# Pairing 64-deep TensorE products in the two halves of the array's rows, in an encoder layer

## The chip, the core and the metric

The kernel runs on one core of one Trainium2 chip: TensorE (PE) for products and transposes, VectorE (DVE), ScalarE (ACT) and GpSimd (POOL) for everything elementwise, SyncE (SP) for issuing most DMAs. Each engine works through its own list of instructions in order and waits on semaphores for the others. The metric is the device time of one execution in microseconds (us); less is better.

## What is computed

One layer: a token mixer made of sparse attention (8 heads, keys chosen by an "indexer") and differential attention (4 heads), then attention into 256 memory tokens, then a mixture of 64 experts. 512 tokens, width 1024, float32. The parts that the change touches:

```python
# indexer: 8 heads of depth 64, one key per token, one weight per query and head
rel    = relu(einsum('bqhd,bsd->bqhs', qib, k_idx) * IDX_DIM ** -0.5)
iscore = einsum('bqh,bqhs->bqs', wib, rel)
_, sel = top_k(iscore, topk)                       # 128 keys for each query
q_lat  = einsum('bqhd,hcd->bqhc', qb, w_uk)        # depth 64, latent of 128
# differential attention: two softmax maps of depth 64 for each of 4 heads
s1 = einsum('bqhd,bshd->bhqs', q1b, k1) * scale + bias
s2 = einsum('bqhd,bshd->bhqs', q2b, k2) * scale + bias
attn = softmax(s1) - lam * softmax(s2)
# mixture of experts: sums start at zero, each expert's rows are added
acc = zeros((n + 1, d)); acc = acc.at[rows].add(yb)
```

## The kernel before

**Products.** For accuracy every float32 operand is split into a high and a low part (`split`: ACT casts the high part, DVE or POOL subtracts to get the low one). A product is then three matmuls into one PSUM bank (`mm3`, L100 to L103): high by high (L101), high by low (L102), low by high (L103).

**Stages.** In order of time: normalisation of the input and its transposes (to about 30 us); 22 projections by 128 columns of `w_in` (thread `dense`, tile `whl` for the split weights) with the indexer's keys and head weights first (`index_keys`), then the four indexer queries `qi0` to `qi3`, the latent, and queries, keys and values of the four differential heads; beside them `index_scores`, `select` (16 rounds of MAX and MATCH_REPLACE on DVE for each of three blocks of queries) and `head_scores`; 16 projections of the memory tokens (`memh`, `meml`) as work between; the sparse attention (`latent_up`, `sparse_scores`, `sparse_out`); output projection, memory attention, routing; from about 600 us the experts, whose weights stream from HBM, three loads of 1024 KB for each of the 64; at the end the sums and a last normalisation.

**Depth 64.** The array has 128 rows and these products need 64. The indexer and the latent fill the other 64 with zeros: `kz` holds the keys once in rows 0 to 63 and once in rows 64 to 127, zeros elsewhere, and `ukz` likewise (both with `fill0`, memsets on DVE); a matmul then uses all rows. `head_scores` gives each of the two maps (`v`) of a head its own half of the rows, without zeros, three matmuls of one half, then, in another step, three of the other.

**Head weights.** The 8 columns of head weights have a projection of their own after that of the keys (tile `ww`, L330, 24 matmuls of 384 columns), then a scale on ACT (`wit`, L331) and three transposes (L335), ahead of the projection of `qi0`.

**Order.** `schedule` (L117) runs the threads as generators. Each step yields two numbers, TensorE time and a delay until the thread's next step may come; the planner keeps a clock from them and calls the first thread that is due. So the program's order comes from these planned numbers; the chip then runs each engine's list in that order, and the tile library adds the waits. A raw weight chunk is loaded two items ahead by SP into one of three buffers and split one item ahead into one of two; eight PSUM banks and six work buffers (`wk`) turn over.

**Zeros.** `clear_sums` stores zeros into the sums in HBM, 12 stores of 256 KB from `zrow`, issued by POOL in one step once the latent's keys (`ckt`) are there. The first scatter into the sums comes after 620 us.

## Time and profile before

| | |
|---|---|
| time, median of 3 runs | 1300.02 us (1300.02, 1294.96, 1300.17) |
| the profiled execution | 1294.74 us, of it 1292.9 us span |
| busy in the span | PE 89%, DVE 58%, ACT 44%, POOL 35% |
| chain that ended last, by engine | PE 33%, DMA 15%, DVE 7% |
| HBM | read 290 MB, written 38 MB |

The span runs from the first to the last instruction; 1.8 us lie around it. "Busy" of PE counts a matmul from its start to a modelled end, and matmuls overlap, so what a matmul costs in a row of them is read from start to start, not from its length. The share of busy time is a mean over stages with different limits: it is read by stretches. The chain that ended last is followed back from the last instruction; it names what each step waited for.

### The profile page before, as it was taken

The numbers are of one execution on the slowest core, as the hardware profiler recorded it, in microseconds if no ns is written. First come the engines' busy times: TensorE is split into PE (matmuls) and PEld (weight loads), VectorE is DVE, ScalarE is ACT, GpSimd is POOL, SyncE is SP. The second block draws the span as 40 slices with busy tenths as digits, with TensorE's granted clock in tenths as the row PEclk, the third lists the DMA queues.
The fourth block names the chain that finished last, engine by engine and source line by source line (L and its number), as shares of the span: only waits on it lengthen the run. The fifth ranks groups of instructions, "written<-read, shape, count | busy, mean of one in ns | idle before, by whom it ended". The sixth has DMA issues, their size and how long they took to land.

```text
span 1292.9 us, 20999 instructions
## 1 busy us (share of the span) xinstructions
PE 1154.6 (89%) x7768; PEld 911.3 (70%) x7768; DVE 752.4 (58%) x1607; ACT 562.6 (44%) x1006; POOL 451.4 (35%) x346
## 2 busy tenths in 40 slices
PE   2999999999899799988999999999999988798870
PEld 2887778898789799877877777777777544454330
DVE  7267995556773747697776767676575311211115
ACT  3234546654554353443555555556464112312122
POOL 4353344552225343363322222222223222222223
PEclk9998999999989899999999999999999988899895
DMA  7352132554416235787999999999999999999985
GB/s 226 81 180 66 49 98 78 143 183 139 144 50 212 61 123 194 252 317 255 312 305 332 345 350 353 348 353 365 363 365 357 348 371 366 358 364 370 374 278 199
DMA packets 138183, 324.09 MB, mean 251 GB/s; under 512 B 13520, under 2 KB 96464, under 8 KB 113248
## 3 DMA queue, kind: packets, MB, share of 16 engines
q1 hardware_dynamic: 120560, 277.93, 59.1%
q0 software_dynamic: 14432, 44.12, 14.1%
q8 instruction: 62, 1.02, 0.3%
q10 hardware_dynamic: 3088, 0.69, 0.2%
q14 instruction: 41, 0.34, 0.1%
HBM read 290.19 MB, written 37.81 MB: 254 GB/s over the span
## 4 chain that ended last, share of the span: by engine, by line
PE 33%; DMA 15%; DVE 7%; issue 3%; ACT 2%; POOL 1%; SPq 0%; DVEq 0%; ACTq 0%; POOLq 0%
PE ps L1360 9%; DMA wraw<-in_e_w_up_dram 6%; PE ps L101 5%; PE ps L102 5%; PE ps L103 5%; DMA wraw<-in_e_w_gate_dram 4%; PE ps L1313 4%; DVE whl L1277 3%; DMA wd<-in_e_w_down_dram 3%; PE ps L1285 2%; PE ps L1324 2%; DMA acc<-y,sidx 1%; PE ps L1226 1%; DVE h2p L202 1%; ACT whl L1276 1%
## 5 line engine op out<-in xcount | busy, mean ns | idle before, releaser
L95 POOL TENSOR_TENSOR whl<-wraw,whl 128x1024 fp32r<-128x1024 f32 x81 | 196.1, 2421 | 265.4 <-ACT whl L94 230.9
L1277 DVE TENSOR_TENSOR whl<-wraw,whl 128x1024 fp32r<-128x1024 f32 x152 | 182.8, 1229 | 65.2 <-ACT whl L1276 64.7
L101 PE MATMUL ps<-whl,xt 128*96 128x256 f32 (+4 forms) x640 | 183.9, 287 | 3.9 <-ACT whl L1276 3.9
L1252 POOL DMA_INDIRECT xg<-rows,sidx x66 | 80.6, 1222 | 297.9 <-PE ps L1301 135.2
L102 PE MATMUL ps<-whl,xt 128*96 128x256 f32 (+4 forms) x640 | 179.2, 280 | 0.6 <-DVE whl L1277 0.6
L103 PE MATMUL ps<-whl,xt 128*96 128x256 f32 (+4 forms) x640 | 179.2, 280 | 0.0
L1276 ACT CAST whl<-wraw 128x1024 fp32r<-128x1024 f32 x152 | 152.4, 1055 | 11.6 <-DMA wraw<-in_e_w_gate_dram 11.3
L1366 POOL DMA_INDIRECT acc<-y,sidx x66 | 97.4, 1476 | 168.2 <-ACT y L1361 113.6
L1360 PE MATMUL ps<-wd,ht 128*96 128x512 f32 (+4 forms) x320 | 145.8, 598 | 2.8 <-DVE ht L1348 1.9
L1313 PE MATMUL ps<-wraw,xn 128*64 128x256 f32 (+1 forms) x832 | 117.1, 404 | 24.4 <-DMA wraw<-in_e_w_up_dram 8.8
L1332 ACT ACTIVATE sg<-ps 64x256 f32<-64x256 f32 (+6 forms) x66 | 25.0, 379 | 242.4 <-PE ps L1313 127.2
L94 ACT CAST whl<-wraw 128x1024 fp32r<-128x1024 f32 x91 | 95.4, 1049 | 56.2 <-PE ps L103 40.5
L101 PEld LDWEIGHTS ps<-whl,xt 128*96 128x96 f32 (+4 forms) x640 | 104.3, 163 | 4.6 <-ACT whl L1276 4.1
L102 PEld LDWEIGHTS ps<-whl,xt 128*96 128x96 f32 (+4 forms) x640 | 104.4, 163 | 1.0 <-DVE whl L1277 0.7
L103 PEld LDWEIGHTS ps<-whl,xt 128*96 128x96 f32 (+4 forms) x640 | 104.2, 163 | 0.3
L1313 PEld LDWEIGHTS ps<-wraw,xn 128*64 128x64 f32 (+1 forms) x832 | 61.2, 139 | 61.1 <-DMA wraw<-in_e_w_up_dram 12.4
L1360 PEld LDWEIGHTS ps<-wd,ht 128*96 128x96 f32 (+4 forms) x320 | 49.3, 163 | 69.9 <-issue 64.6
L1348 DVE COPY ht<-ps 128x128 f32<-128x128 f32 (+6 forms) x66 | 21.4, 324 | 94.2 <-PE ps L1346 94.1
L1361 ACT COPY y<-ps 96x512 f32<-96x512 f32 (+4 forms) x80 | 46.6, 583 | 67.7 <-PE ps L1360 67.5
L1337 DVE SCALAR_TENSOR_TENSOR hm<-ps,og,sg 64x256 f32<-64x256 f32 (+4 forms) x54 | 36.8, 682 | 60.4 <-ACT sg L1332 47.9
L101 PE MATMUL ps<-xTh,whl 128*128 128x512 f32 (+1 forms) x168 | 66.6, 396 | 0.0
L102 PE MATMUL ps<-xTl,whl 128*128 128x512 f32 (+1 forms) x168 | 64.8, 386 | 0.0
(420 smaller groups left out, 2780.4 us busy)
## 6 DMA issues: line engine op xcount, KB each, us to landing
wraw<-in_e_w_gate_dram SPq DMA_DIRECT2D x64, 1024.0 KB, 23.3
wraw<-in_e_w_up_dram SPq DMA_DIRECT2D x64, 1024.0 KB, 24.2
wd<-in_e_w_down_dram SPq DMA_DIRECT2D x64, 1024.0 KB, 23.2
wraw<-in_w_in_dram SPq DMA_DIRECT2D x21, 512.0 KB, 3.8
wraw<-in_m_wkv_dram SPq DMA_DIRECT2D x16, 512.0 KB, 4.3
wraw<-in_m_wq_dram SPq DMA_DIRECT2D x16, 512.0 KB, 4.0
wraw<-in_m_wo_dram SPq DMA_DIRECT2D x16, 512.0 KB, 4.0
wraw<-in_w_o_dram SPq DMA_DIRECT2D x12, 512.0 KB, 3.5
```

Source lines behind the costliest of these rows:

```text
L94: nc.scalar.copy(hi, src)
L95: eng.tensor_sub(lo, src, hi.bitcast(F32))
L101: nc.tensor.matmul(ps, lhsT=a, rhs=b, start=start, stop=False)
L102: nc.tensor.matmul(ps, lhsT=a, rhs=bl, start=False, stop=False)
L103: nc.tensor.matmul(ps, lhsT=al, rhs=b, start=False, stop=stop)
L1252: nc.gpsimd.indirect_dma_start(out=xg[0:n, :], out_offset=None, in_=rows, in_offset=bass.IndirectOffsetOnAxis(ap=gi[0:n, :], axis=0), boun ...
L1276: nc.scalar.copy(hi[v], w[i][v])
L1277: lo_eng.tensor_sub(lo[v], w[i][v], hi[v].bitcast(F32))
L1313: nc.tensor.matmul(ps[HALF * i:HALF * i + n, 0:256], lhsT=xt[:, k, 0:n], rhs=w[i][:, k, :], start=k == 0, stop=k == KD - 1)
L1360: nc.tensor.matmul(ps[0:n, :], lhsT=ht[:, j, 0:n], rhs=wd[:, j, cs], start=j == 0, stop=j == 1)
L1361: nc.scalar.copy(y[0:n, cs], ps[0:n, :])
L1366: nc.gpsimd.indirect_dma_start(out=accs[(NB - m) % 2], out_offset=bass.IndirectOffsetOnAxis(ap=si[0:n, :], axis=0), in_=y[0:n, :], in_offs ...
```

## The change

1. A new helper `mm3_halves` takes two products, one for each half of the rows, and issues their six matmuls in turn: half 0, half 1, half 0, ... into two banks. `index_scores` (two heads at a time), `head_scores` (both maps of a head) and `latent_up` (two heads) use it.
2. The indexer's keys are kept once in rows 0 to 63 (`kd`) and copied to rows 64 to 127 by a DMA on POOL's queue; `uk` holds two heads in the two halves. The zeros of `kz` and `ukz` go, and half of their splits' instructions.
3. The keys' projection has 72 columns: 64 of keys and the 8 head weights. The separate projection of head weights goes. `index_split` splits two halves of 4 x 72 columns, with the low parts on DVE.
4. The zeros are stored by SP's queue, one store a step, with a planned delay of 1.5 us between them.
5. The planned numbers of these threads change with the steps, and with them the order of everything up to the memory attention.

```diff
+    def mm3_halves(pss, ops):
+
+        for i, j in ((0, 2), (0, 3), (1, 2)):
+            for ps, op in zip(pss, ops):
+                nc.tensor.matmul(ps, lhsT=op[i], rhs=op[j], start=i + j == 2, stop=i == 1)
+
+    HALVES = (slice(0, 64), slice(64, 128))
...
     def index_split(raw):
...
-        for j in range(2):
-            js = slice(j * 64, (j + 1) * 64)
-            split(hl[:, 0, :, js], hl[:, 1, :, js], raw[:, :, 0:64], lo_eng=nc.vector if j else nc.gpsimd)
-        ww = wk([P, 2, KD, 8], F32R, name="ww")
-        split(ww[:, 0], ww[:, 1], raw[:, :, 64:72])
+        for k in (slice(0, 4), slice(4, 8)):
+            split(hl[:, 0, k, 0:72], hl[:, 1, k, 0:72], raw[:, k, :])
...
     def index_keys(wh, wl):
...
-        yield from proj(ps, wh, wl, xt)
-        kz = slot([P, 2, 2, SEQ], F32R, name="kz")
...
-        fill0(kz[64:128, :, 0, :])
-        fill0(kz[0:64, :, 1, :])
-        for v in range(2):
...
-            split(kz[r, 0, v, :], kz[r, 1, v, :], ps[r, :])
...
-        yield from proj(psw[0:8, 0:384], KW[0][:, 0], KW[0][:, 1], xt, P, SEQ)
-        nc.scalar.activation(wit[0:8, :], psw[0:8, 0:384], AF.Copy, scale=float(A_HEADS) ** -0.5)
+        yield from proj(ps[0:72, :], wh[:, :, 0:72], wl[:, :, 0:72], xt)
+        kd = slot([P, 2, SEQ], F32R, name="kd")
...
+        split(kd[0:64, 0, :], kd[0:64, 1, :], ps[0:64, :])
+        nc.gpsimd.dma_start(kd[64:128, :, :], kd[0:64, :, :])
...
+        nc.scalar.activation(wit[64:72, :], ps[64:72, P:SEQ], AF.Copy, scale=float(A_HEADS) ** -0.5)
...
     def index_scores():
...
-                ps = bank()
-                mm3(ps[:, 0:w], qih[:, h // 2, q0:q0 + P], qil[:, h // 2, q0:q0 + P],
-                    kz[:, 0, h % 2, 0:w], kz[:, 1, h % 2, 0:w], True, True)
+                if h % 2 == 0:
+                    pss = [bank()[:, 0:w] for _ in range(2)]
+                    mm3_halves(pss, [(qih[r, h // 2, qs], qil[r, h // 2, qs], kd[r, 0, 0:w], kd[r, 1, 0:w])
+                                     for r in HALVES])
+                ps = pss[h % 2]
...
-                yield 3 * w / 2400, w / 1500
+                if h % 2:
+                    yield 3 * w / 2400, 2 * w / 1500 + w / 1000
...
     def head_scores():
...
-                    mm3(ps[:, 0:w], QK[h][r, 0, 0, q], QK[h][r, 0, 1, q], QK[h][r, 1, 0, 0:w], QK[h][r, 1, 1, 0:w],
-                        True, True)
...
+                mm3_halves([ps[:, 0:w] for ps in pss],
+                           [(QK[h][r, 0, 0, q], QK[h][r, 0, 1, q], QK[h][r, 1, 0, 0:w], QK[h][r, 1, 1, 0:w])
+                            for r in HALVES])
...
     def latent_up(u):
...
-                for v in range(2):
...
-                    mm3(ps[:, 0:256], UW["uk"][:, 0, h, :], UW["uk"][:, 1, h, :], qa[:, 0, :], qa[:, 1, :], True, True)
...
+                mm3_halves(pss, [(UW["uk"][r, 0, a, :], UW["uk"][r, 1, a, :], qa[r, 0, :], qa[r, 1, :]) for r in HALVES])
...
     def clear_sums():
...
-            nc.gpsimd.dma_start(accs[0][SEQ:, cs], zrow)
+            nc.sync.dma_start(accs[0][SEQ:, cs], zrow)
             for t in range(NT + 1):
-                nc.gpsimd.dma_start(accs[1][t * P:(t + 1) * P, cs], zrow)
+                nc.sync.dma_start(accs[1][t * P:(t + 1) * P, cs], zrow)
+                yield 0.0, 1.5
```

The order at three places. TensorE's list where the last block of index scores (`kz`, or `kd`) is computed, with the PSUM tiles' numbers; before, beside the head scores (`qk`):

```order
L101 MATMUL ps_1006<-qk_759 128x384
L102 MATMUL ps_1006<-qk_759 128x384
L103 MATMUL ps_1006<-qk_759 128x384
L101 MATMUL ps_1016<-kz_306,qi_346 128x512
L102 MATMUL ps_1016<-kz_306,qi_346 128x512
L103 MATMUL ps_1016<-kz_306,qi_347 128x512
L101 MATMUL ps_1023<-qk_759 128x384
```

and now, with a projection (`whl`) behind it:

```order
L109 MATMUL ps_751<-kd_303,qi_315 128x512
L109 MATMUL ps_752<-kd_303,qi_315 128x512
L109 MATMUL ps_751<-kd_303,qi_315 128x512
L109 MATMUL ps_752<-kd_303,qi_315 128x512
L109 MATMUL ps_751<-kd_303,qi_316 128x512
L109 MATMUL ps_752<-kd_303,qi_316 128x512
L101 MATMUL ps_737<-xTh_145,whl_667 128x512
```

The two heads alternate between two banks, and the index scores no longer run beside the head scores: their last pair stands behind 240 projection matmuls (`xTh` and `xTl`) in place of 324, ahead of the first head score.

ScalarE's list behind the projection of the indexer's keys, where `wit` is the scaled head weights that TensorE transposes before it goes on; before:

```order
L94 CAST kz<-ps 64x512
L94 CAST whl<-wraw 128x1024
L94 CAST kz<-ps 64x512
L331 ACTIVATE wit<-ps 8x384
L94 CAST qi<-ps 128x384
```

and now:

```order
L94 CAST kd<-ps 64x512
L94 CAST whl<-wraw 128x1024
L331 ACTIVATE wit<-ps 8x384
L94 CAST qi<-ps 128x384
L94 CAST whl<-wraw 128x1024
```

One cast went; the split of the next weights still stands ahead of `wit`, and what TensorE did meanwhile, the projection of the head weights, is gone.

VectorE's list in the second block of index scores (`dsel<-rl` adds one head's part; MAX and MATCH_REPLACE are a round of the selection for the first block; `at`, `t` are head scores); before:

```order
L366 SCALAR_TENSOR_TENSOR dsel<-rl,widx,dsel 128x384 x2
L394 ISA at,m_887<-ps,dsel 128x128
L394 ISA m_887 128x1
L399 RECIPROCAL r_891<-s_889 128x1
L394 ISA t_904,m_905<-ps,dsel 128x128
L394 ISA m_905 128x1
L366 SCALAR_TENSOR_TENSOR dsel<-rl,widx,dsel 128x384
```

and now:

```order
L368 SCALAR_TENSOR_TENSOR dsel<-rl,widx,dsel 128x384
L382 MAX m_833<-dsel 128x8
L368 SCALAR_TENSOR_TENSOR dsel<-rl,widx,dsel 128x384
L383 MATCH_REPLACE dsel<-m_833,dsel 128x256
L382 MAX m_864<-dsel 128x8
L383 MATCH_REPLACE dsel<-m_864,dsel 128x256
L382 MAX m_891<-dsel 128x8
L368 SCALAR_TENSOR_TENSOR dsel<-rl,widx,dsel 128x384
```

Before, all 16 rounds for the first block stand in one piece after 14 of the 24 additions, and the last additions lie between head scores. Now additions and rounds alternate, with 24 rounds ahead of the last addition (23 before), and no head score lies among them.

## Rows read from the trace of the kernel before

**Rows 1.** Stretches: length, PE, PEld, DVE, ACT, POOL busy, PEclk, DMA share, GB/s.
```profile
43.50:199.40 155.90, 150.94 (x707) 122.50 (x706) 112.55 (x270) 67.31 (x129) 69.10 (x44) 0.98 0.33 95
...
257.00:430.00 173.00, 161.16 (x1194) 152.56 (x1193) 111.87 (x272) 85.78 (x180) 69.41 (x31) 0.96 0.44 143
430.00:600.00 170.00, 151.70 (x1150) 142.79 (x1150) 116.50 (x224) 68.37 (x124) 73.70 (x51) 0.96 0.57 193
600.00:1000.00 400.00, 396.02 (x2759) 312.35 (x2760) 279.25 (x500) 224.41 (x336) 114.44 (x107) 1.00 1.01 346
1000.00:1250.00 250.00, 214.53 (x1462) 115.93 (x1462) 50.78 (x151) 54.99 (x115) 62.59 (x52) 0.94 1.02 365
```
**Rows 2.** The chain that ended last: start, length in us, what.
```profile
1053.92 25.31 DMA wraw<-in_e_w_gate_dram
```
**Rows 3.** Timeline of PE, 241 to 242.5 us: start, length, line, form.
```profile
241.05 0.28 PE L102 MATMUL ps<-meml,whl 128*128 128x256 f32 x1
241.17 0.28 PE L103 MATMUL ps<-memh,whl 128*128 128x256 f32 x1
241.38 0.44 PE L101 MATMUL ps<-qk 64*128 64x384 f32 x1
241.66 0.33 PE L102 MATMUL ps<-qk 64*128 64x384 f32 x1
241.83 0.33 PE L103 MATMUL ps<-qk 64*128 64x384 f32 x1
242.09 0.38 PE L101 MATMUL ps<-memh,whl 128*128 128x256 f32 x1
242.31 0.28 PE L102 MATMUL ps<-meml,whl 128*128 128x256 f32 x1
```
**Rows 4.** The chain again, expert stage: whole-array products, half-column products, transposes.
```profile
620.38 0.87 PE ps L1285 x8
...
1006.47 3.59 PE ps L1360 x8
...
1015.17 1.72 PE ps L1324 x8
```
**Rows 5.** Head weights' projection: duration ns min/median/max, first and last start.
```profile
L103 PE MATMUL ps<-xTh,ww x8: 332/336/338, 38.7 to 42.3; 128*8 128x384 f32 x8
```
**Rows 6.** Timeline of ACT behind the keys' projection.
```profile
38.73 0.58 ACT L94 CAST kz<-ps 64x512 fp32r<-64x512 f32 x1 [7.66 <-PE ps L103]
39.22 1.05 ACT L94 CAST whl<-wraw 128x1024 fp32r<-128x1024 f32 x1
...
42.72 0.48 ACT L331 ACTIVATE wit<-ps 8x384 f32<-8x384 f32 x1 [1.84 <-PE ps L103]
```
**Rows 7.** Timeline of PE, the transposes of the head weights.
```profile
43.25 0.35 PE L335 MATMUL ps<-ident,wit 8*128 8x8 f32 x3 [0.57 <-ACT wit L331]
```
**Rows 8.** Timeline of DVE, normalisation of the input.
```profile
21.49 0.74 DVE L188 SCALAR_TENSOR_TENSOR x<-x,rs,gb 128x512 f32<-128x512 f32 x1
...
25.51 3.57 DVE L188 SCALAR_TENSOR_TENSOR x<-x,rs,gb 128x512 f32<-128x512 f32 x2
```
**Rows 9.** Timeline of POOL in the same stretch.
```profile
23.32 1.72 POOL L95 TENSOR_TENSOR kw<-wraw,kw 128x512 fp32r<-128x512 f32 x1
...
25.54 2.34 POOL L95 TENSOR_TENSOR whl<-wraw,whl 128x1024 fp32r<-128x1024 f32 x1
```
**Rows 10.** DVE in two stretches, all instructions: length, busy, PEclk, DMA share.
```profile
67.70:144.40 76.70, 60.03 (x138) 0.96 0.35 104
144.40:192.50 48.10, 46.81 (x118) 1.00 0.28 84
```
**Rows 11.** The same, of tile dsel alone (additions and rounds).
```profile
67.70:144.40 76.70, 51.08 (x104) 0.96 0.35 104
```
**Rows 12.** Timeline of POOL, five of the twelve stores of zeros.
```profile
82.98 2.67 POOL L967 DMA_DIRECT2D acc<-zrow  x5
```
**Rows 13.** SP's stores to the sums later: issue ns, first and last start.
```profile
L1417 SPq DMA_DIRECT2D acc<-so x8: 319/320/331, 586.5 to 603.6; - x8
```

More of the change, by code (lines that the diff above doesn't have):

```diff
@@ L495, in head_scores @@
                 pr = []
-                for v in range(2):
-                    r = slice(64 * v, 64 * v + 64)
-                    q = slice(i * P, (i + 1) * P)
-                    ps = bank()
-                    mm3(ps[:, 0:w], QK[h][r, 0, 0, q], QK[h][r, 0, 1, q], QK[h][r, 1, 0, 0:w], QK[h][r, 1, 1, 0:w],
-                        True, True)
+                q = slice(i * P, (i + 1) * P)
+                pss = [bank() for _ in range(2)]
+                mm3_halves([ps[:, 0:w] for ps in pss],
+                           [(QK[h][r, 0, 0, q], QK[h][r, 0, 1, q], QK[h][r, 1, 0, 0:w], QK[h][r, 1, 1, 0:w])
+                            for r in HALVES])
+                for v, ps in enumerate(pss):
                     t1 = at[:, OFF[i]:OFF[i + 1]] if v == 0 else wk([P, 512], name="t2")[:, 0:w]
                     pr.append((t1, soft(t1, ps, nd[:, 512 - w:512], w, sl)))
-                    yield 3 * w / 2400, w / 1000 + 0.1
+                yield 3 * w / 2400, 2 * w / 1000 + 0.2 + w / 800
                 (p1, r1), (p2, r2) = pr
@@ L538, in latent_w @@
         UW["uv"] = slot([P, 2, A_HEADS, P], F32R, name="uvz")
-        UW["uk"] = slot([P, 2, A_HEADS, P], F32R, name="ukz")
-        uvz, ukz = UW["uv"], UW["uk"]
+        UW["uk"] = slot([P, 2, 4, P], F32R, name="uk")
+        uvz, uk = UW["uv"], UW["uk"]
         ukr = wk([P, A_HEADS, 64], name="ukr")
@@ L556, in latent_w @@
         yield 0.5, 1.0
+        split(uk[:, 0], uk[:, 1], ps)
         for v in range(2):
             r = slice(64 * v, 64 * v + 64)
-            split(ukz_p[r, 0, :, v, :], ukz_p[r, 1, :, v, :], ps[r, :, :])
             split(uvz_p[:, 0, :, v, r], uvz_p[:, 1, :, v, r], uvr_p[:, :, v, :])
@@ L598, in latent_up @@
                 yield 0.0, 0.8
-                for v in range(2):
+                pss = [bank()[:, 0:256] for _ in range(2)]
+                mm3_halves(pss, [(UW["uk"][r, 0, a, :], UW["uk"][r, 1, a, :], qa[r, 0, :], qa[r, 1, :]) for r in HALVES])
+                for v, ps in enumerate(pss):
                     h = 2 * a + v
-                    ps = bank()
-                    mm3(ps[:, 0:256], UW["uk"][:, 0, h, :], UW["uk"][:, 1, h, :], qa[:, 0, :], qa[:, 1, :], True, True)
-                    split(QL[u, g][:, h % 4, 0, :], QL[u, g][:, h % 4, 1, :], ps[:, 0:256], scale=0.125 * 2.0 ** (h + 1))
-                    yield 0.35, 0.2
+                    split(QL[u, g][:, h % 4, 0, :], QL[u, g][:, h % 4, 1, :], ps, scale=0.125 * 2.0 ** (h + 1))
+                yield 0.35, 0.4
     PA = {}
```

16 lines of the change are left out of this document (5 added, 11 removed).

## The prediction

> **What bounds the kernel now.** I first cut the span into stretches and set each engine's busy time beside the DMA share [rows 1]. From 600 to 1250 us the DMA engines are at 1.01 and 1.02 of their time, and the chain that ended last waits there for expert weights, 25 us at a time [rows 2]: this part has a fixed amount of data to move and ends when it began plus that. It begins with the first expert loads, which the program puts behind steps of the memory attention (FIRST_LOADS); in the 170 us ahead of 600 the DMA share is only 0.57 [rows 1], so no queue of transfers hides when they start. A microsecond saved ahead of 600 us is therefore worth a microsecond at the end, and all edits lie there. From 43.5 to 199.4 us PE is busy for 150.9 of 155.9 us, from 257 to 430 for 161.2 of 173 [rows 1]: PE bounds the front, so I count PE time, from start to start, and look for what else is nearly full. That is DVE: 46.8 of 48.1 us from 144.4 to 192.5, though only 60.0 of 76.7 just before [rows 10].
>
> **What a product of 64 rows costs.** [Rows 3] show one group of three with 384 columns amid whole-array products of 256. In steady state the starts lie 0.12 us apart for 256 columns and 0.17 for 384. Around the group there are four longer steps: 0.21 into it (0.12 without the change), 0.28 behind its first (0.17), 0.26 out of it (0.17), 0.22 behind the next whole-array product (0.12). Together 0.09 + 0.11 + 0.09 + 0.10 = 0.39 us for each visit to the 64-row shape. By the same slope I take 0.23 us for 512 columns, and for 128, where I have no row of such a product, the 0.12 of 256 as a ceiling. One group of three is then 0.36, 0.36, 0.51 and 0.69 us for 128 to 512 columns.
>
> **Do two halves run at once?** No row shows two halves of the rows back to back. The nearest are two halves of the columns: eight products of 512 columns in the two column halves take 1.72 us, eight over the whole width 3.59 [rows 4]. I take the same halving for the rows, and keep as the other end that the halves queue up one behind the other. Between them lies a limit by the weights: eight transposes of 128 columns take 0.87 us, 0.11 each [rows 4], so if each half's weights have to be loaded in turn, a pair of matmuls takes at least 0.22.
>
> The Trainium skill (TensorE: Matmul & The Clock Gate, Part 3: Packing small matmuls — row/col tiling) says that products in different row groups run concurrently, starting some 4 ns apart, and gives 3.07 times for four row tiles, short of four. By an estimate from that ratio (0.77 of the ideal) the pairs below would save about 5 us less. No run here shows it yet.
>
> **Pairs, the sum.**
> Head scores: 4 heads, 4 widths, 2 maps. Before, 32 groups: 8 x (0.36 + 0.36 + 0.51 + 0.69) = 15.4 us, and 32 visits x 0.39 = 12.5; after, 7.7 and 16 visits, 6.2. Saved 14.0.
> Index scores: before, 8 x (0.36 + 0.51 + 0.69) = 12.5 with no visits, since the zeros make them whole-array; after, 6.2 and 12 visits, 4.7. Saved 1.6.
> Latent: before, 16 x 0.36 = 5.8; after, 2.9 and 8 visits, 3.1. Lost 0.2.
> Together 15.4 us off PE; most of it is 16 visits fewer and the maps' overlap. If weights load in turn, 7.2 of it goes (0.10 for each step of 128 or 256 columns, 0.05 of 384). If the halves queue up, the sum is 6.3 - 4.7 - 3.1 = 1.5 us lost.
>
> **Keys and head weights.** The 24 matmuls of 384 columns go; by [rows 5] eight thirds of them span 3.6 us, 0.17 each, so 4.0 us. The matmul of 72 columns in place of 128 streams the same 512 and saves nothing. But that projection covered ACT: now PE's next work, the transposes of the scaled head weights, waits for a cast of the keys (0.58), the split of the next weights (1.05), which still stands ahead, and the scale (0.48) [rows 6], about 2.1 us where it waited 0.57 [rows 7]. That takes 1.5 back. Ahead of it, POOL no longer makes a low part of the keys' weights (1.72 us, with the next split of 2.34 behind [rows 9]); beside these, two DVE instructions on the last rows of the input take 3.57 us where one alone takes 0.74 [rows 8]. TensorE's first projection waits for them: between 0 and 1.7 us earlier, I take 1.2. Net 3.7.
>
> The copy of the keys to the other half stands in POOL's list ahead of the split for the second indexer query: cast 0.58, low part about the same, issue 0.53 (a fifth of 2.67 [rows 12]), then 2.34 of split: 4 us behind the keys, and PE needs it after 2.1 us of waiting and 24 x 0.17 = 4.1 us of the first query. Covered, with 2 us to spare. If the longer wait drops PE to 1.2 GHz, as the mean clocks 0.98 and 0.96 say happens in the front [rows 1], I allow 3 us, on the upper end.
>
> **Zeros.** POOL loses 12 x 0.53 = 6.4 us of issuing [rows 12], SP gains 12 x 0.32 = 3.8 [rows 13]. Nine stores stand ahead of the load of one chunk, which is needed two items (2 x 24 x 0.23 = 11 us) later; the stores' 3.1 MB are 9 us of transfers at the 346 GB/s of [rows 1]. I put it at nothing, and 2 us on the upper end. The memsets that go had DVE to themselves while it waited for projections: nothing.
>
> **What DVE takes back.** The new order packs the index scores between 12 projection matmuls each: from the first pair to the last PE has 11 x 12 x 0.23 + 10.9 = 41 us of work. Between the same points DVE has all 24 additions and 24 rounds; before, with 23 rounds, those took 51 us of busy time [rows 11] out of 60 [rows 10] and had 76.7 us to fit. So DVE is some 10 us short. PE can run ahead by what six work buffers hold of relus (one of them now held longer by the zeros), two or three pairs or 7 to 11 us. Lost between 0 and 10; I take 4, since the run-ahead covers most.
>
> **Sum.** 15.4 + 3.7 - 4 = 15.1 us. On the profiled execution's 1294.74 us: 1279.6. The median shown is 1300.02, with one of the three runs at 1294.96, so the profiled one is of the faster kind; 5.3 us on top give 1284.9. I forecast the middle, 1282.
>
> One thing I don't count: the last head scores now stand behind 144 instead of 216 of the 384 memory-key products, so 72 x 0.12 = 8.6 us of free work moves into the sparse attention, where PE is idle for 11.8 us [rows 1]. At best it fills half, 6 us.
>
> **Rivals.**
> *DVE is the bound up to the end of the selection.* For it: 97% from 144 to 192 us [rows 10]; against: over 67.7 to 192.5 together DVE has 107 us of work in 125. All 10 us lost instead of 4, and 4 more where head scores wait for a full DVE: 1287 to 1292. The Trainium skill (TensorEngine Tiling (Array Packing), Performance Considerations) warns of just this: tiling speeds up TensorE and not the emptying of PSUM. The trace so far agrees in the 97%.
> *The halves queue up.* Nothing in the rows speaks for it but that no row shows the overlap. 3.7 - 1.5 = 2.2 us saved: 1292.5 to 1298.
> *Each change of half stalls like a change of shape.* Six alternations in a pair mean five changes; at the 0.20 us that entering the shape costs [rows 3], 36 pairs x 5 x 0.20 = 36 us on top of the queueing: 1294.7 + 36 + 1.5 - 3.7 = 1329, to 1334 on the median. It decides from 0.05 us a change on (9 us, 0.5% slower net). The Trainium skill (TensorEngine Tiling (Array Packing), Tiling Modes, Key Properties) says that changing the mode drains TensorE and changing just the tile does not; rows 3 bear out the first, no row the second.
> *The end does not follow the front,* because transfers begin on another event than I think: 1300.
>
> **How the numbers follow.** Forecast (1272 to 1287) 0.62; something better through the sparse stage 0.04; DVE 0.13, four fifths of it still over 0.5% below 1300; queueing 0.10; stalls 0.07; end not following 0.04. A measurement can tell about 0.5% from no change: 1293.5 and 1306.5. Faster 0.62 + 0.04 + 0.10 = 0.76, same 0.15, slower 0.09 (the stalls and an order that turns out bad). The range runs from 1270 (sum without DVE's 4 and with the 6 of the sparse stage) to 1297, queueing on the slower kind of run; it leaves out the stalls and little else.
>
> **What would show it.** In the new profile: the two matmuls of a pair starting within 0.02 us, and a pair of 512 columns every 0.23 us (queueing: 0.46; stalls: more); a wait of some 2 us ahead of L335; the first memory-key product some 13 us earlier than before; the DVE busy share from 60 to 120 us above 90%; the first expert loads and the whole of what follows shifted by the same 15 us, with the stretch from there to the end unchanged in length. I am wrong if that last length changes, or if PE shows new waits for DVE between 60 and 190 us that add up to over 10 us.

## The result, and the profile after

| | before | after |
|---|---|---|
| median | 1297.25 us (20 runs, 1292.58 to 1300.84) | 1286.99 us (20 runs, 1283.75 to 1295.83) |
| the profiled execution, of it span | 1294.74, 1292.9 us | 1286.77, 1285.0 us |

The ratio is 0.9935, 95% interval 0.9921 to 0.9949: some 8.4 us faster. (The medians alone are 10.3 us apart; the ratio, which the argument uses, is close to that of the means.) 1282 was forecast, 1270 to 1297 as the range. The time is in the range and the sign is right, but it is also 1287.0, where the rival "DVE is the bound up to the end of the selection" begins. Which of the two mechanisms gave it is the question of this part.

The stretches of [rows 1], now, same columns:

```profile
43.50:199.40 155.90, 147.28 (x732) 115.59 (x731) 112.56 (x289) 70.77 (x145) 65.57 (x33) 0.96 0.34 98
257.00:430.00 173.00, 159.82 (x1192) 151.44 (x1192) 110.42 (x272) 83.23 (x177) 69.56 (x31) 0.96 0.47 149
430.00:600.00 170.00, 157.38 (x1200) 149.16 (x1198) 119.71 (x221) 71.92 (x123) 75.16 (x52) 0.96 0.62 207
600.00:1000.00 400.00, 394.60 (x2743) 309.20 (x2743) 274.21 (x496) 219.41 (x331) 113.74 (x106) 1.00 1.01 346
1000.00:1250.00 250.00, 213.14 (x1439) 113.96 (x1437) 50.28 (x149) 56.84 (x118) 64.93 (x53) 0.93 1.00 356
```

From 600 us on little changed but the start: the chain that ended last still waits there for expert weights (below, against [rows 2]), and from the first expert product to the end it is 676.9 us, 676.2 before. One of those waits:

```profile
1086.64 25.47 DMA wraw<-in_e_w_up_dram
```

The front is where to look. Timeline of PE, one pair of 512 columns between whole-array products (start, length, line, form; "x6" are the pair's six matmuls together):

```profile
93.11 0.39 PE L103 MATMUL ps<-xTh,whl 128*128 128x512 f32 x1
93.43 0.96 PE L109 MATMUL ps<-kd,qi 64*128 64x512 f32 x6
94.33 0.50 PE L101 MATMUL ps<-xTh,whl 128*128 128x512 f32 x1
```

Six matmuls take 0.90 us from first start to the next product, three times 0.23 and the visit. In the trace's single records the two halves start mostly 3 to 4 ns apart. The halves run at once, and a pair costs what one group of three did in [rows 3].

Timelines of PE and ACT behind the keys' projection, against [rows 6, 7]:

```profile
40.56 0.35 PE L335 MATMUL ps<-ident,wit 8*128 8x8 f32 x3 [2.13 <-ACT wit L331]
```

```profile
38.47 0.58 ACT L94 CAST kd<-ps 64x512 fp32r<-64x512 f32 x1 [8.24 <-PE ps L103]
38.96 1.04 ACT L94 CAST whl<-wraw 128x1024 fp32r<-128x1024 f32 x1
40.02 0.48 ACT L331 ACTIVATE wit<-ps 8x384 f32<-8x384 f32 x1
```

The wait of 2.13 us is the 2.1 forecast. The transposes come at 40.6 us for 43.2, 2.6 earlier for a forecast of 3.7: the first projection begins 0.8 earlier, not 1.2, and takes 9.0 us for 8.4.

Then the gain goes. The first memory-key product comes at 198.57 us for 202.5, only 4 us sooner where 13 were forecast. Part of that is order: 66 of the 96 head-score products now stand ahead of it, 54 before, so PE's work up to there fell by only 7.5 us (150.1 to 142.6, worked out as below).

**The balance of the front.** From the transposes of the head weights to the last product of the memory attention's output (om), one row each for before and after (from:to, length, then busy time and count of PE, PEld, DVE, ACT, POOL, then PEclk, DMA share, GB/s):

```profile
43.20:543.70 500.50, 472.51 (x3119) 425.38 (x3120) 326.95 (x781) 239.68 (x483) 208.63 (x120) 0.97 0.42 130
```

```profile
40.60:538.10 497.50, 463.27 (x3118) 415.30 (x3119) 320.27 (x776) 234.95 (x482) 205.75 (x110) 0.96 0.43 133
```

Length less PE busy is PE's idle time: 28.0 us before, 34.2 after. The granted clock falls to 1.2 GHz for 27.3 us in all before and for 41.0 after, by the steps of the clock in the two traces; half of that is counted as lost, 13.7 and 20.5 us (some of it is time in which PE waited anyway; with PE's busy time alone the losses are 12.0 and 19.2 us, and work and clock below would be -16.4 and +7.2). What is left is work at 2.4 GHz: 458.8 before, 442.8 after. So:

| part | forecast | measured |
|---|---|---|
| keys and head weights, up to their transposes | -3.7 | -2.6 |
| PE's work in pairs | -15.4 | -16.0 |
| waits of PE | +4 (put down to DVE) | +6.2 |
| the lower clock behind waits | 0 (3 on the upper end) | +6.8 |
| routing, up to the first expert product | 0 | -3.0 |
| experts and end | 0 | +0.7 |
| sum | -15.1 | -7.9 |

The profiled spans differ by 7.9 us. The saving is all there and 13.0 us of it are given back. One execution's clock may be chance, but the mean granted clock over the executions says the same: 0.9629 in 91 of before, 0.9586 in 20 of after, which on their times is 48 and 53 us lost. So the executions bear out some 5 of the 6.8 us.

Routing is set apart because it takes 68.6 to 75.6 us over the fourteen profiled kernels without an edit there. Two profiles of one program differ by as much: after and e3_gap, whose engines run the same instructions in the same order (below), take 70.0 and 75.5. So its -3.0 is chance as far as is known. Below, kernels are therefore also compared at the last om product.

### The profile page after: what moved, and what is told of

Its sections match the earlier page's. It is cut to its first block, busy times and chain, and to the rows that moved or that the text cites. A ratio compares the mean times of both kernels' runs of the same rounds, so it can differ in the third digit from the quotient of the medians.

```text
span 1285.0 us, 20951 instructions
## 1 busy us (share of the span) xinstructions
PE 1141.7 (89%) x7744; PEld 898.9 (70%) x7744; DVE 740.6 (58%) x1599; ACT 557.2 (43%) x1003; POOL 444.8 (35%) x334
## 4 chain that ended last, share of the span: by engine, by line
PE 27%; DMA 18%; issue 6%; DVE 5%; POOL 2%; ACT 2%; SPq 0%; POOLq 0%; ACTq 0%; DVEq 0%
PE ps L1361 8%; DMA wraw<-in_e_w_up_dram 6%; DMA wd<-in_e_w_down_dram 6%; PE ps L101 4%; PE ps L102 4%; PE ps L103 4%; PE ps L1314 2%; DMA wraw<-in_e_w_gate_dram 2%; DVE whl L1278 2%; DMA acc<-y,sidx 2%; PE ps L1286 1%; PE ps L1325 1%; PE ps L1227 1%; DMA h<-acc 1%; POOL whl L95 1%
## 5 line engine op out<-in xcount | busy, mean ns | idle before, releaser
L1338 DVE SCALAR_TENSOR_TENSOR hm<-ps,og,sg 64x256 f32<-64x256 f32 (+4 forms) x54 | 36.8, 681 | 62.4 <-ACT sg L1333 49.4
L101 PE MATMUL ps<-xTh,whl 128*128 128x512 f32 (+1 forms) x168 | 69.1, 411 | 0.9 <-ACT whl L94 0.9
L103 PE MATMUL ps<-xTh,whl 128*128 128x512 f32 (+1 forms) x168 | 66.2, 394 | 4.1 <-POOL whl L95 4.1
```

What stands on the lines that cost most here:

```text
L101: nc.tensor.matmul(ps, lhsT=a, rhs=b, start=start, stop=False)
L103: nc.tensor.matmul(ps, lhsT=al, rhs=b, start=False, stop=stop)
```

## The experiments

| kernel | ratio to before, 95% | first memory key | last om | PE work | PE idle | lost to clock |
|---|---|---|---|---|---|---|
| before | 1 | 202.5 | 543.7 | 458.8 | 28.0 | 13.7 |
| after | 0.9935 [0.9921, 0.9949] | 198.6 | 538.1 | 442.8 | 34.2 | 20.5 |
| e1_heads | 1.0004 [0.9979, 1.0029] | 211.5 | 550.7 | 444.7 | 39.8 | 22.2 |
| e2_seq | 0.9946 [0.9927, 0.9965] | 195.7 | 535.6 | 443.5 | 34.2 | 17.1 |
| e3_gap | 0.9953 [0.9930, 0.9976] | 196.5 | 536.9 | 443.0 | 33.8 | 20.5 |
| e4_uk | 0.9860 [0.9836, 0.9883] | 198.2 | 531.4 | 442.3 | 30.1 | 18.8 |
| e5_heads_uk | 1.0000 [0.9979, 1.0021] | 211.8 | 546.0 | 447.9 | 34.5 | 20.5 |
| e6_before_uk | 0.9978 [0.9956, 1.0001] | 198.7 | 538.9 | 458.2 | 26.2 | 11.9 |
| e7_same | 0.9953 [0.9933, 0.9974] | 199.9 | 540.2 | 458.5 | 26.8 | 13.7 |
| e8_sel | 0.9975 [0.9951, 0.9999] | 196.5 | 533.1 | 444.1 | 37.7 | 10.2 |
| e9_half | 0.9889 [0.9855, 0.9923] | 190.6 | 525.6 | 443.6 | 30.8 | 10.2 |
| e10_half_same | 0.9983 [0.9958, 1.0007] | 199.1 | 540.8 | 460.4 | 28.1 | 11.9 |
| e11_zpool | 0.9952 [0.9931, 0.9974] | 197.2 | 534.1 | 443.6 | 36.8 | 11.9 |
| e12_best | 0.9980 [0.9959, 1.0000] | 202.3 | 544.9 | 443.2 | 38.0 | 23.9 |

Times in us, of the profiled execution; work, idle and clock as in the balance. A profiled execution can lie at an edge of its kernel's runs (e8_sel's is its fastest of 12, e4_uk's its slowest of 7), so the ratio decides where the two differ. The rows of after and e3_gap are two measurements of one program: 0.0018 in the ratio, 2.1 us at the first memory key and 1.2 us at the last om product mean nothing by themselves.

**First theory and rival.** A: the order of the index stage fills DVE from 75 to 150 us and the loss is there. B: a faster PE finds operands late and falls to the lower clock wherever time is saved. Four kernels came first.

**e1_heads**: the kernel before with `head_scores` in pairs, nothing else.

```diff
-                    mm3(ps[:, 0:w], QK[h][r, 0, 0, q], ...
-                    yield 3 * w / 2400, w / 1000 + 0.1
+                mm3_halves([ps[:, 0:w] for ps in pss], ...
+                yield 3 * w / 2400, 2 * w / 1000 + 0.2 + w / 800
```

> The kernel before with one part of the change alone: the head scores in pairs (both maps of a head in turn in the two halves of the rows); index scores, latent, keys and zeros as before. By the sum this is 14.0 us of the 15.4 us of the pairs. Theory A (what was lost of the gain was lost in the index stage, whose new order fills DVE from 75 to 150 us): this kernel keeps the old index stage and is 11 to 14 us faster than before, 0.989 to 0.9915, so faster than the whole change (0.9935). Rival B (a PE that is done sooner finds splits and loads late and drops to the lower clock more often, wherever the saving is made): 5 to 8 us, 0.994 to 0.996. Rival C (the order of the head scores matters more than their length): slower than 0.997.

No gain at all: 1.0004. PE's work fell by 14.1 us, just the 14.0 of the sum, and idle time and clock took back 20.3 ahead of the last om product (routing is 4.4 us shorter here, which hides part of that in the ratio). Theory A had placed the loss in the changed index stage, which this kernel doesn't have; yet DVE is full here too, only later (DVE's is the third busy time):

```profile
125.00:150.00 25.00, 22.16 (x104) 17.15 (x103) 24.73 (x57) 12.73 (x26) 7.94 (x4) 0.93 0.20 54
150.00:175.00 25.00, 20.22 (x96) 16.35 (x95) 24.43 (x69) 11.04 (x27) 7.04 (x4) 0.87 0.16 43
175.00:200.00 25.00, 25.00 (x130) 19.75 (x130) 24.32 (x69) 14.99 (x33) 13.77 (x7) 1.00 0.34 106
```

So either B, or DVE without regard to the index order. (The planned numbers of this step changed too, and with them the order of the lists: 72 of the 96 head-score products stand ahead of the first memory key here.)

**e2_seq**: the changed kernel, the halves one behind the other.

```diff
-        for i, j in ((0, 2), (0, 3), (1, 2)):
-            for ps, op in zip(pss, ops):
+        for ps, op in zip(pss, ops):
+            for i, j in ((0, 2), (0, 3), (1, 2)):
```

> The changed kernel with the two halves of each pair one behind the other (three matmuls of half 0, then three of half 1) in the same places and with the same number of visits to the 64-row shape; only the overlap of the halves is taken away. By the steps of the profile the overlap is worth 7.7 us in the head scores, 6.2 in the index scores and 2.9 in the latent. Theory A (the overlap is real, but in the index stage DVE decides): 8 to 12 us above the changed kernel, 1.000 to 1.003 of before. If all of it counts: 16 to 17 us above, 1.006. Rival (the two halves would overlap without being alternated, or the gain came from fewer visits alone): within 3 us of the changed kernel, 0.9935 to 0.996.

The rival held: 0.9946, and PE's work is that of after. The trace shows why, a pair of 512 columns:

```profile
91.99 0.97 PE L109 MATMUL ps<-kd,qi 64*128 64x512 f32 x6
92.89 0.50 PE L101 MATMUL ps<-xTh,whl 128*128 128x512 f32 x1
```

0.90 us as in after: the second half's three matmuls run beside the first half's three, some 10 ns behind each. The kernel doesn't take the overlap away and so doesn't measure it; e7_same does.

**e3_gap**: `SEL_GAP = 1.2` becomes `2.4`.

> The changed kernel with the planned gap between two rounds of the selection doubled (SEL_GAP 2.4 for 1.2), which draws the same DVE work of the selection out over a longer stretch, among projections and head scores. Theory A (DVE is the bound from 75 to 150 us, and PE's waits of 0.7 to 2.3 us and the lower clock there come from it): these waits go, the first memory-key product comes 3 to 6 us sooner, and the time is 3 to 6 us below the changed kernel, 0.989 to 0.991. Rival B (those waits are for POOL's and ACT's splits of weights, or DVE's work is only moved on to the head scores, where PE waits for it instead): 0.992 to 0.996, no nearer to the sum.

Nothing learned of DVE, for the edit changed nothing: in the two traces every engine runs the same instructions in the same order, and the rounds ran from 78 to 159 us, as in after (79 to 160). So this is a second measurement of the changed kernel, 0.9953 beside 0.9935. Moving the rounds took a dependency (e8_sel).

**e4_uk**: one line behind the loads in `latent_w`.

```diff
+        yield 0.0, 4.0
```

> The changed kernel with a planned delay of 4 us between the loads of the latent's up-weights (ukr, uvr) and their transposes. In the changed kernel PE waits 3.75 us there for the transfer and then runs at 1.2 GHz for 6.8 us, which costs some 3.4 more. Theory B (single waits on late operands and the lower clock behind them took the gain back): this wait and the low clock go, 3 to 7 us below the changed kernel, 0.988 to 0.991. Rival A (the index stage took it, and what is won here is lost again at the next wait for head scores): within 2 us of the changed kernel, 0.992 to 0.995.

0.986, the fastest of all kernels here: about 9.7 us below after. In after PE waits 3.75 us at 210 us for the transfer of the up-weights, which the new order issues too late; before, it waited 1.2 (wait list of before: total, times, longest; then the timeline of after):

```profile
PE ps L550 <- DMA ukr<-in_a_w_uk_dram: 1.2, 1, 1.2
```

```profile
213.97 0.45 PE L552 MATMUL ps<-ident,ukr 128*128 128x128 f32 x1 [3.75 <-DMA ukr<-in_a_w_uk_dram]
```

From 205 to 225 us before, after and e4_uk:

```profile
205.00:225.00 20.00, 19.28 (x137) 17.16 (x136) 10.63 (x31) 11.21 (x24) 9.49 (x5) 1.00 0.27 82
```

```profile
205.00:225.00 20.00, 16.08 (x112) 14.96 (x113) 8.93 (x34) 10.27 (x26) 9.39 (x5) 0.83 0.39 98
```

```profile
205.00:225.00 20.00, 19.84 (x163) 18.58 (x163) 13.87 (x47) 14.13 (x37) 12.20 (x6) 1.00 0.52 129
```

The wait and the clock of 0.83 are gone, and the last om product comes 6.7 us sooner; the line moved other work too (from here on the lists differ from those of after). That is for B. Two controls:

**e5_heads_uk** and **e6_before_uk**: the same line in e1_heads and in the kernel before.

> The kernel before with the head scores in pairs (as e1_heads, which was no faster than before) and with a planned delay of 4 us between the loads of the latent's up-weights and their transposes. In e1_heads PE waits 3.9 us there for the transfer and 10.2 us at 1.2 GHz follow. Theory B (the 14 us that PE saves are real, and single waits with the lower clock behind them take them back): the wait and the low clock go, 3.9 + 5.1 = 9 us below e1_heads, 0.992 to 0.995 of before. Rival (what the head scores save is taken back elsewhere whatever is mended, say by DVE under the selection): 0.998 to 1.001, as e1_heads.

> The kernel before with nothing but the planned delay of 4 us between the loads of the latent's up-weights and their transposes. In the kernel before PE does not wait there. Theory B (the delay helps only where a wait stands): no change, 0.998 to 1.002. Rival (the delay is good by itself, by the order of what follows, and so says nothing of the pairs): 0.992 or less.

e6_before_uk lies at the edge of no change (0.9978), where only the wait of 1.2 us stood. But e5_heads_uk gains nothing over e1_heads, though the same wait of 3.9 us is gone there. In its profile the last om product does come 4.7 us sooner (546.0 for 550.7), and routing, at 73.1 us for 68.6, takes 4.5 of it back. One profile can't say that this holds over the executions, so why the same line is worth 9.7 us in one kernel and nothing in the other is open. The single wait isn't shown to be the general cause.

**e7_same**: the changed kernel, both products of each pair in one half of the rows (so the second map, head or key copy isn't computed). Every engine's list is that of after.

```diff
-    HALVES = (slice(0, 64), slice(64, 128))
+    HALVES = (slice(0, 64), slice(0, 64))
```

> The changed kernel with both products of each pair read from the lower half of the rows (the second map, head or key copy is replaced by the first, so the output is not the reference's); every instruction, its size and its place stay, but the two products of a pair can't run at once. By the steps of the profile the overlap is worth 7.7 us in the head scores, 6.2 in the index scores and 2.9 in the latent, 16.8 together, if a pair without it takes twice the time. Theory A and B alike: PE's net work grows by 15 to 17 us. If all of that counts: 1.006 of before. Theory B (a later PE finds fewer operands late, as the faster one found more): part of it only, 1.000 to 1.003. Rival (two products in one half of the rows cost no more than in two): 0.9935.

Now the overlap is gone; a pair of 512 columns takes 1.59 us for 0.90:

```profile
97.21 1.66 PE L109 MATMUL ps<-kd,qi 64*128 64x512 f32 x6
98.80 0.50 PE L101 MATMUL ps<-xTh,whl 128*128 128x512 f32 x1
```

PE's work is 15.7 us more than in after. The ratio is 0.9953 for 0.9935, the last om product 2.1 us later: of 15.7 us saved by the overlap, some 2 reach the end, no more than after and e3_gap differ by. In place of work, after has 7.4 us more idle and loses 6.8 more to the clock. And most of what the change gains comes without the overlap (0.9953): in the profile 2.0 us from the keys, 1.2 from smaller waits and 4.3 in the routing stage, which varies, less 2.8 behind it.

**e8_sel**: the selection of the second and third block made to wait for the transposed values of a head.

```diff
+            if i > 1:
+                nc.vector.tensor_scalar(isc[0:64, w - 64:w], VB[i - 2][0:64, i - 2, 0, 0:64].bitcast(F32), 0.0, -1e38,
+                                        op0=OP.mult, op1=OP.add)
```

> The changed kernel with the selection of the second block of queries begun only when the first differential head's values are transposed (about 137 us in the changed kernel), that of the third at the second head's: one small DVE instruction on each block makes the rounds depend on it. e3_gap left the rounds where they were (78 to 159 us); here some 20 us of DVE work leave the stretch from 100 to 137 us. Theory A (DVE is the bound there, and through ACT, whose exponentials wait for DVE ahead of the splits, also makes POOL's low parts of the weights late): PE's waits of 2.3, 1.9 and 2.2 us at 115, 130 and 140 us shrink by 4 us or more together, with 3 us or more of the low clock: 0.987 to 0.990 of before. Rival (the same waits come up where the rounds now lie, 140 to 200 us): 0.992 to 0.996.

0.9975, slower than after and than either expectation. DVE's work left 100 to 125 us and filled 125 to 200; after and then e8_sel:

```profile
100.00:125.00 25.00, 22.67 (x102) 16.99 (x100) 24.42 (x52) 6.28 (x10) 9.09 (x5) 0.93 0.25 68
125.00:200.00 75.00, 69.01 (x344) 53.30 (x343) 57.25 (x162) 41.81 (x94) 34.84 (x18) 0.95 0.27 78
```

```profile
100.00:125.00 25.00, 22.68 (x108) 17.32 (x108) 11.66 (x27) 10.49 (x22) 10.41 (x6) 1.00 0.26 68
125.00:200.00 75.00, 66.80 (x336) 51.91 (x336) 71.28 (x196) 38.55 (x86) 31.74 (x17) 0.95 0.28 80
```

DVE is at 11.7 of 25 us and then at 71.3 of 75, and PE waits at 171, 190 and 195 us in place of 130 and 140. As the rival had it, moving the work moves the waits (the profiled execution is its fastest of 12, so its clock says little). What tells A from B is to take it away.

**e9_half** and **e10_half_same**: 8 rounds of the selection for 16 (64 keys chosen in place of 128), with and without the overlap.

```diff
-            for r in range(TOPK // 8):
+            for r in range(TOPK // 16):
```

> The changed kernel with 8 rounds of the selection in place of 16 for each block (64 keys chosen in place of 128, so the output is not the reference's), which takes some 20 us of DVE work out of the stretch from 79 to 160 us and moves none of it elsewhere (e8_sel only moved it, and the waits moved along). Theory A (DVE decides the length up to about 150 us, through ACT, which waits 23 us for DVE's softmax work there in the changed kernel and 12.5 in e7_same): ACT's waits for DVE fall below 12 us, the first memory-key product comes 5 to 9 us sooner (at 190 to 194 us), the time is 0.985 to 0.990 of before. Rival B (waits and lower clock arise wherever PE is made faster, with or without DVE): no sooner than 196 us, 0.992 to 0.995.

> As e9_half, and both products of each pair from the lower half of the rows as in e7_same, so that they can't run at once (not the reference's output either). With 16 rounds the overlap's 16 us of PE work made no difference to the first expert product (608.1 us with it, 608.9 without). Theory A (it was hidden by DVE): with half the rounds it shows, the first memory-key product 8 to 11 us and the first expert product 8 to 16 us later than in e9_half, 0.993 to 1.000. Rival B: again no difference, within 3 us of e9_half.

With e7_same and after this makes a square (ratio; last om product). PE, ACT and POOL run the same lists in all four, and within a row of the table DVE does too, so order is no rival for the last column:

| | overlap | no overlap | the overlap is worth |
|---|---|---|---|
| 16 rounds | 0.9935; 538.1 | 0.9953; 540.2 | 0.0018; 2.1 us |
| 8 rounds | 0.9889; 525.6 | 0.9983; 540.8 | 0.0094 (12 us); 15.2 us |

The rows of e7_same, e9_half and e10_half_same for the whole front, as those of before and after above:

```profile
41.20:540.20 499.00, 472.16 (x3118) 426.41 (x3119) 314.46 (x776) 235.73 (x482) 204.46 (x110) 0.97 0.43 133
```

```profile
40.90:525.60 484.70, 453.86 (x3118) 408.27 (x3119) 295.09 (x704) 234.60 (x482) 205.13 (x110) 0.98 0.44 137
```

```profile
40.40:540.80 500.40, 472.32 (x3118) 425.73 (x3119) 293.91 (x704) 235.95 (x482) 204.33 (x110) 0.98 0.43 133
```

With half the rounds the overlap's work counts nearly in full (15.2 of 16.7 us), with all of them 2.1, which can't be told from nothing. By the ratios it is 12 us, give or take 5, beside 2, give or take 3. And without the overlap, taking 20 us from DVE (314.5 to 293.9 busy) is worth nothing (540.2 and 540.8). So PE's work and DVE's stood side by side, and taking from one alone was worth little.

Where it happens is plainest up to the first memory-key product, as the selection ends ahead of it. The same rows up to there, after, e7_same, e9_half, e10_half_same:

```profile
40.60:198.60 158.00, 149.38 (x742) 117.76 (x742) 111.94 (x288) 70.19 (x144) 67.46 (x35) 0.96 0.34 99
41.20:199.90 158.70, 156.46 (x741) 126.68 (x741) 106.21 (x288) 71.21 (x144) 66.51 (x35) 0.98 0.34 98
40.90:190.60 149.70, 145.57 (x742) 116.24 (x742) 86.97 (x216) 70.44 (x144) 66.91 (x35) 0.98 0.36 104
40.40:199.10 158.70, 156.46 (x741) 126.68 (x741) 85.63 (x216) 71.31 (x144) 66.53 (x35) 0.98 0.34 98
```

| up to the first memory-key product | length | PE work | PE idle | lost to clock |
|---|---|---|---|---|
| after | 158.0 | 142.6 | 8.6 | 6.8 |
| e7_same | 158.7 | 153.1 | 2.2 | 3.4 |
| e9_half | 149.7 | 142.2 | 4.1 | 3.4 |
| e10_half_same | 158.7 | 153.1 | 2.2 | 3.4 |

With 16 rounds the overlap saves 10.5 us of work there and 9.8 go to waits and clock; with 8 rounds it saves 10.9 and 1.9 go. PE's waits for POOL's part of the weights' split, from 43 to 200 us, are none in e7_same, 4.1 us in after and 0.9 in e9_half. In after:

```profile
PE ps L103 <- POOL whl L95: 4.1, 2, 2.2
```

Behind that product the four have about the same idle time (25.6, 24.6, 26.7, 25.8 us). What differs there is the clock (13.7, 10.2, 6.8, 8.5 us lost), and no run ties that to DVE: the same two waits of PE in the sparse attention, 1.6 and 2.3 us, are followed by 6.8 us at 1.2 GHz in after, e3_gap and e10_half_same, and by none in e7_same and e9_half. Over all executions, by span and mean granted clock, the clock took 53.4, 49.2, 47.1 and 48.6 us, and what is left of the span is 1233.5, 1240.7, 1231.8 and 1242.2. So without the clock the overlap is worth 7.2 us with 16 rounds and 10.4 with 8; the lower clock takes back 4.1 of the 7.2 and nothing of the 10.4. (The four were not timed side by side, and before itself lost 46 to 50 us to the clock in the sets that they were timed with.)

Theory A stands in this form: the load of the rounds hides the overlap, partly by waits and partly by the lower clock; by the ratios it hides 10 us, give or take 6. That the additions and the softmax take part is likely from the trace below, but no run varied them. B is right that waits bring a lower clock, but it expected the loss with or without DVE's load, and with half the rounds there is little. One expectation missed: ACT's waits for DVE fell to 18.6 us, not below 12, so they are no measure of the loss by themselves.

**e11_zpool**: the zeros issued by POOL again.

> The changed kernel with the twelve stores of zeros issued by POOL in one step, as before the change. The prediction put this part at nothing, 2 us at most. Expected: within 2 us of the changed kernel, 0.992 to 0.995. Rival (the stores stand ahead of weight loads on SP's queue and of what follows): 0.990 or less. Rival (POOL's 6.4 us of issuing delay its splits): 0.997 or more.

0.9952 beside 0.9935: within 2.2 us, and within what after and e3_gap differ by. SP's issues cost more than the 0.32 of [rows 13]:

```profile
L967 SPq DMA_DIRECT2D acc<-zrow x10: 426/620/872, 87.7 to 95.7; - x10
```

0.62 us each, and no engine waits for them. This part is worth nothing that was measured here.

**e12_best**: three waits mended at once.

```diff
-        nc.scalar.activation(wit[64:72, :], ps[64:72, P:SEQ], AF.Copy, scale=float(A_HEADS) ** -0.5)
+        nc.vector.tensor_scalar(wit[64:72, :], ps[64:72, P:SEQ], float(A_HEADS) ** -0.5, None, op0=OP.mult)
...
+            yield 0.0, 2.5
+            sl = 2.0 ** (-2.0 * (h + 1))
...
+        yield 0.0, 4.0
```

> The changed kernel with three waits mended: the delay of 4 us ahead of the transposes of the latent's up-weights (e4_uk, 0.986), the scale of the head weights on DVE and ahead of the split of the keys (ACT's cast of the next weights no longer stands ahead of it; 2.1 us of wait and 3.4 us of lower clock), and a planned delay of 2.5 us ahead of the first scores of each head (2.3 us of wait for the keys' low part, 3.4 us of lower clock). If all of it counts: 2.1 + 1.7 + 2.3 + 1.7 = 8 us below e4_uk, 0.980. Theory A (DVE has to get through its work up to 150 us either way): the waits come back as others, 0.984 to 0.988.

0.998, worse than either expectation. The waits for the head weights (0.6 us for 2.1) and at 114 us went, but head scores begun later met DVE's backlog: PE waits 5.4 us for DVE at the transposes of the scores, which is 0.4 in after. Which of the three edits did it wasn't taken apart; but e4_uk's line, which alone had given 0.986, is among them, so what the mending of single waits gains doesn't add up.

## Why the prediction was right and where it was not

**How DVE's load reaches PE.** The wait list of PE names DVE hardly at all in this stretch, which misled me both before and after. In after the first softmax step of the first head stands in DVE's list behind the rounds; the pair it reads was done at about 117.3 us. Timelines of DVE, ACT, POOL and PE in order:

```profile
125.97 0.56 DVE L382 MAX8 m<-dsel 128x8 f32<-128x384 f32 x1
126.44 0.27 DVE L397 CUSTOM_DVE_ANT_0 at<-ps,dsel 128x128 f32<-128x128 f32 x1
```

```profile
126.76 0.40 ACT L400 ACTIVATE at<-at,m 128x128 f32<-128x128 f32 x1 [13.10 <-DVE m L397]
...
128.35 1.04 ACT L94 CAST whl<-wraw 128x1024 fp32r<-128x1024 f32 x1
```

```profile
129.47 2.57 POOL L95 TENSOR_TENSOR whl<-wraw,whl 128x1024 fp32r<-128x1024 f32 x1 [12.65 <-ACT whl L94]
```

```profile
132.10 0.50 PE L103 MATMUL ps<-xTh,whl 128*128 128x512 f32 x1 [1.92 <-POOL whl L95]
```

ACT's exponential waits 13.10 us for DVE, the cast of the next weights stands behind it, POOL's low part waits 12.65 for the cast, and PE waits 1.92 for POOL. The wait list puts that down to POOL. ACT's waits for DVE from 75 to 150 us, before, after and e7_same (total, times, longest):

```profile
ACT at L397 <- DVE m L394: 4.5, 2, 3.5
```

```profile
ACT at L400 <- DVE m L397: 23.4, 3, 13.1
```

```profile
ACT at L400 <- DVE m L397: 12.5, 4, 4.7
```

And DVE in the same 75 us, before and after:

```profile
75.00:150.00 75.00, 71.28 (x314) 55.96 (x313) 62.01 (x148) 33.85 (x67) 33.36 (x26) 0.95 0.33 99
```

```profile
75.00:150.00 75.00, 66.95 (x298) 48.23 (x297) 73.24 (x184) 27.66 (x54) 26.91 (x14) 0.93 0.33 99
```

62.0 of 75 us before, 73.2 after. Half the rounds bring it back to what it was before; e9_half:

```profile
75.00:150.00 75.00, 71.44 (x341) 53.36 (x341) 61.98 (x147) 33.17 (x69) 30.55 (x16) 0.98 0.38 111
```

**Point by point.**
- *Do two halves run at once:* right, and in full; neither the limit by the weights nor a stall at each change of half shows. The cost of a visit was right too: for a pair of 512 columns 0.69 + 0.39 = 1.08 us were forecast, and it takes 0.09 more than usual into it, 0.90 for it and 0.10 more behind it.
- *Pairs, the sum:* right as PE work, 16.0 us for 15.4 (e1_heads: 14.1 for 14.0; e7_same: 15.7 for 16.8 by the overlap).
- *Keys and head weights:* the wait was right (2.13 us for 2.1), the net 1.1 us too high.
- *Zeros:* right, e11_zpool.
- *What DVE takes back:* the step that failed. I had the right shortage ("some 10 us short") and then took 4, "since the run-ahead covers most". The work buffers let PE's index pairs run ahead of DVE's additions; they do nothing for the head scores' softmax behind the rounds, nor for the casts behind ACT's exponentials. Up to the first memory-key product half the rounds bring 8.3 us back (158.0 to 149.7), 4.5 in waits and 3.4 in clock; there the term is twice what I took. Of the 13.0 us given back against before, the rest lies behind that product and isn't shown to be DVE's.
- *A wait that no term had:* the new order issues the transfer of the latent's up-weights late, 3.75 us of waiting for 1.2, with the lower clock behind it. Mending it gave 6.7 us at the last om product (e4_uk), and it stands in e9_half too.
- *DVE's list before:* less changed than I wrote ahead of the prediction. In the trace of before, three of the first block's rounds already stand among the additions, and the other 13 follow the twelfth addition, not the fourteenth. The count of rounds ahead of the last addition (23 and 24) is right.
- *The clock:* I priced it for one wait, at 3 us on the upper end. It is over half of what was given back: 6.8 of 13.0 us in the profile, some 5 us over the executions. In the profile 6.8 us of lost clock came with 6.2 us of new waiting; that is no price, as the same wait is followed by the lower clock in one kernel and not in another.
- *The rivals:* DVE as the bound, at 0.13, is nearest to what the square shows. Its range begins at 1288 if its sum is done again (1282 and the 6 us more that it loses), so the measured 1287.0 lies between it and the forecast and decides nothing. The Trainium skill (TensorEngine Tiling (Array Packing), Performance Considerations, PSUM Bottleneck) warns that tiling speeds up TensorE and not the emptying of PSUM. The square shows the like for DVE's load (2.1 us with 16 rounds, 15.2 with 8), but not for PSUM: the rounds that it takes away read none, and no run varied the reading of PSUM.
- *What would show it:* the pair starts and the wait ahead of L335 came as forecast, and the last stretch kept its length; the first memory-key product (4 us for 13) didn't. DVE was busy for 49.4 us from 60 to 120 us, 82% where over 90% was forecast; the full stretch came later, 98% from 75 to 150. The first expert load was issued 15 us sooner (512.9 to 498.0), those behind it between 5 and 32, and from the 21st to the 50th 7 to 9, near the 7.9 of the span. "New waits for DVE that add up to over 10 us" was the wrong test: by the wait list those between 60 and 190 us even fell, from 3.2 to 0.3. PE's waits grew by 6.2 us in all and bear other engines' names, and the clock hid the rest.
- That the time fell into the range is partly luck: the range takes in any saving from 3 to 30 us, and errors cancel. 3.0 us of the 7.9 are the routing stage's, which varies, and most of the gain needs no overlap (e7_same, 0.9953), though the overlap was most of the sum.

What stays open: why e4_uk's line gains 9.7 us in the changed kernel and nothing in e5_heads_uk; what decides whether a wait is followed by the lower clock; and how much of the loss behind the first memory-key product is DVE's.

## What to carry over

Before pricing a saving on one engine, look for the engine that is next in the same stretch and follow the in-order lists across engines: a full DVE showed as ACT waiting, then POOL late, then PE waiting "for POOL". To learn whether a second limit hides a saving, take work away from each of the two engines, alone and together; each alone may be worth nothing. Moving the second engine's work (e8_sel) or mending several waits at once (e12_best) may only move the waits; mending one (e4_uk) can also pay, and only a run tells. Measure one program twice before reading a difference of 2 us: an edit that turned out to change nothing (e3_gap) gave that scale here.

## What the runs showed of the hardware

- **Matmuls of two row halves needn't alternate.** In e2_seq's program three matmuls of one half stand ahead of three of the other, and the six take 0.90 us as when they alternate (1.59 in one half). They start in pairs, mostly 10 ns apart, so the second half's first matmul starts ahead of the first half's second. The Trainium skill (PSUM — Partial Sum Buffer, Engine vs sequencer instructions) says that matmuls start and complete in program order; across row halves this run shows otherwise, and the measurement decides. In the kernel before the two maps stood in separate steps with other products between; by e2_seq, putting them side by side should have been enough.
- **No loss in packing two halves.** The Trainium skill (TensorE: Matmul & The Clock Gate, Part 3: Packing small matmuls — row/col tiling) gives 3.07 times for four row tiles. The estimate drawn from it, 5 us less, doesn't hold for two: a pair of 512 columns with its visit takes 1.09 us for the 1.08 worked out without such a loss, and the work saved was 16.0 us for 15.4.
- **One DVE instruction, 0.70 or 3.11 us.** In the routing stage the same instruction, after and e9_half:

```profile
582.19 0.70 DVE L1221 TENSOR_TENSOR oh<-place,posf 128x512 fp32r<-128x512 bf16 x1
```

```profile
571.26 3.11 DVE L1221 TENSOR_TENSOR oh<-place,posf 128x512 fp32r<-128x512 bf16 x1
```

In e9_half POOL subtracts a weight chunk from 571.45 for 2.37 us beside it; in after it begins one only at 583.44, and works on a smaller tile beside DVE:

```profile
571.45 2.37 POOL L95 TENSOR_TENSOR whl<-wraw,whl 128x1024 fp32r<-128x1024 f32 x1
```

```profile
582.22 1.26 POOL L1401 TENSOR_TENSOR hs<-hm,hs 128x256 fp32r<-128x256 f32 x1
```

[Rows 8, 9] look alike. So the long time goes with POOL's split of a chunk and not with any work of POOL; that the two get in each other's way is suggested by this, not shown. It may be part of why routing takes 68.6 to 75.6 us with one order of instructions.
